# Two-layer encoder trunk: where the second layer's memory keys and values are projected

## Chip, core and metric

The kernel runs on one core of a Trainium2 chip. The metric is device time in microseconds (us) of one execution; three runs of the kernel before gave 1487.01, 1487.39 and 1491.83 us, a median of 1487.39 us. A profiled execution stands beside them. TensorE (PE) is the matrix engine, VectorE (DVE), ScalarE (ACT) and GpSimd (POOL) are the elementwise engines, and SyncE (SP) issues the DMAs named here.

## What is computed

Two pre-norm layers on 1024 tokens of width 1024. Each layer projects its normalised input to queries, keys, values and gates, attends over the tokens, attends over 256 memory tokens with 4 heads of 128, gates, projects out and adds the residual. The part that the change touches is the memory's:

```python
memn = rmsnorm(mem, mem_norm_gain)            # (1, 256, 1024)
for l in range(DEPTH):                        # 2 layers
    mk, mv = jnp.split(memn @ w_mem_kv[l], 2, axis=-1)   # 4 heads of 128 each
    ...
    ym = memory_attn(qm, mk, mv)
```

Both layers use the same normalised memory with their own 1024x1024 weights. So the second layer's `mk` and `mv` depend on nothing of the first layer and can be made at any time before the second layer's memory attention.

## The kernel before

**Arithmetic.** All matmuls are fp32r. An fp32 operand is split in two: a high part (a rounded copy, ACT) and a low part (the operand less its high part, DVE or POOL), and each product is three matmuls: high x high, high x low, low x high. Weights come in units of 256 KB (128 x 512 fp32): a load into a `wraw` buffer (four of them), a copy to `wh`, a subtraction to `wl` (four of each; `wload`, `wunit`, `wparts`, lines 135 to 161). With `wsplit = ("act", "both")` the subtractions go to DVE and POOL in turn (`either`, L1284). One unit feeds 12 matmuls of 256 columns (keys) or 6 of 512 columns (values).

**Stages.** *prep* (`project_a`, L936) loads the tokens and the memory, scales them by the gains and splits them, projects A-attention's keys, values and queries and rotates them (`rope`, L857), and takes the rows' root mean squares from a second copy of the tokens (`stats`, L809, tiles `xt`). It also projects both layers' memory keys and values: first layer `mem_keys` L987 and `mem_values` L989, second layer L1003 and L1014 (the matmuls are recorded at L561 for keys and at L590 for values, for both layers). These use the memory times its gain but not yet divided by its root mean square; that factor (`rows_m` along columns, `rs_m` along rows) is applied when the results are evicted (L570, L597), and the high and low parts are stored to `kvd[0]` and `kvd[1]` in HBM. *l0* is the first layer's attention, *out0* its output projection. *front*, the stage of sums (L1550), projects the second layer's inputs by a Winograd scheme: pairs of 128 output columns with seven products of 12 matmuls (x, z, then y, x, y, x, z; all recorded at L1619), whose weights are sums and differences of four 256 KB quarters (tiles `wq`, eight buffers; L1667) and whose results are added up in tiles `P` (six buffers) and stored through `yb` (two buffers) or, for gates, directly. Ten pairs go in the order 0, 1, 2, 4, ..., 9, 3; the first four have x and z done early, so that pair 3, the last, has five products left. *l1* is the second layer's attention; it loads `kvd[1]` head by head (`odd`, L2006, recorded as `k<-kv` at L1021), and its matmuls are kept in program order. *out1* ends the kernel.

**What sets the order.** Instructions are put in order on each engine before the run by a scheduler that simulates the engines: it goes by program order, raised by the offsets in `AHEAD` (in *front* weights are raised by 100, evictions by 500, sinks by 20), and by when it believes operands to be ready. At run time every engine, and SP's DMA queue, works in that fixed order. A tile of a tag takes its buffers in turn, so the next tile waits until the oldest buffer's last reader is done.

Of the kernel before, what the change touches and what calls it, by code (L numbers as in the profile page):

```python
# [9 lines left out]
F32 = mybir.dt.float32  # L10
F32R = mybir.dt.float32r
I32 = mybir.dt.int32
AF = mybir.ActivationFunctionType
OP = mybir.AluOpType
# [6 lines left out]
KT = 8  # L21
MEM = 256
EPS = 1e-6
NEG = -1e30
UNIT = 4
PLAN = "xv.xx.V1V1V2V1V1V1V2V1V1V1V2V1V1V1V2V1x2z2V1V1V2V1V1V1V2V1V1V1V2V1V1V1V2V1z4z2z2"
# [21 lines left out]
            c=(("P", "P"), ("P", "P"), ("P", "P"), ("yb", "yb"))),  # L48
       dict(y=(("P", "P", "q", "q", "v"), ("k", "k", "k", "k", "q", "q"), ("H",) * 6, ("H",) * 6, ("P", "P", "q", "q", "v"),
               ("k", "k", "k", "k", "q", "q"), ("H",) * 6),  # L50
            c=(("H", "H"), ("H", "H"), ("mk", "sg"), ("yb", "yb"))))
# [13 lines left out]
class Trunk:  # L65
# [61 lines left out]
    def split(self, h, l, src):  # L127
        self.copy(h, src)
        self.nc.vector.tensor_tensor(l, src, h, op=OP.subtract)
# [805 lines left out]

    def project_a(self, qa, ks, v, qd, mem_h, kvd):  # L936

# [33 lines left out]
        for i in range(9):  # L971
            nc.tensor.matmul(p[i % 2], warm[:, :128], warm, start=True, stop=True)
        w0, w1m = io["w_mem0"], io["w_mem1"]
        mem_l = self.st("mem", [128, KT, MEM], F32R, pool=self.xp)
# [11 lines left out]
        self.wsplit = ("act", "dve")  # L986
        end = [self.mem_keys(w0, mem, kvd[0], ("pj", "tr"), "so", "rt1")]  # L987
        self.wsplit = ("act", "both")
        end.append(self.mem_values(w0, mem, kvd[0], "so"))  # L989
        self.rope_tables()  # L990
# [6 lines left out]
        self.loaded = None  # L997
        self.along_columns(self.rows_m, self.rs_m)
        for e in end:
            e()  # L1000
        for q in range(2):
            after(self.k_unit(units[q], q, ks, v))
        self.mem_keys(w1m, mem, kvd[1], ("tr", "tr"), "so", "rt1")()  # L1003
        self.stats(range(4, 8))
# [6 lines left out]
        for q in range(4):  # L1011
            after(self.q_unit(self.a_unit(w2, q), q, 2, qa, qd))
            if q == 1:
                self.mem_values(w1m, mem, kvd[1], "so")()  # L1014
        while late:
# [533 lines left out]

    def front(self, w, pairs, order, values, plan, x1, squares, dests):  # L1550

# [3 lines left out]
        nc, tc = self.nc, self.tc  # L1555
# [90 lines left out]
        def finish(x, z, n1, tag, e=v):  # L1646

            with self.ahead("evict" if tag == "wq" else "sink"):
# [3 lines left out]
                end(n1, 0, c, e)  # L1652

        def raw(j):
            raw = [self.st("wq", [128, 512]) for _ in range(4)]
            with self.ahead("w"):
                for i, t in enumerate(raw):
                    nc.sync.dma_start(t, w[pairs[j][i // 2]][:, 512 * (i % 2):512 * (i % 2) + 512])
            return raw
# [58 lines left out]
        early = len(xs)  # L1718
        for j in order:
            n1, n2 = pairs[j]  # L1720
            if j:
# [41 lines left out]
    def build(self):  # L1763
        nc, tc, io = self.nc, self.tc, self.io
        with ExitStack() as ctx:
# [17 lines left out]
            def dram(n, name, shape=(128, T)):  # L1783
                return [self.dr.tile(list(shape), F32, name=f"{name}{k}") for k in range(n)]
# [5 lines left out]
            self.vec = nc.vector  # L1790
            kvd = dram(2, "kv", (4, 128, 4, MEM))
            x1d = dram(8, "x1_")
            qd = self.dr.tile([4, 2, 128, T], F32, name="qa")
# [16 lines left out]
            with self.phase("prep", ("act", "dve"), "right", p_pj=5, p_tr=3, rp=2, so=4, x=6, xt=3, rt1=2, rt2=1, rqn=1,  # L1810
                            rss=3, ah=4, al=4, xv=3, xp=2, q=4, k=4):
                self.pools = {"q": early}
                with tc.tile_pool(name="start", bufs=1, reuse_waits="tile", side="right") as self.xp:
                    mq = self.project_a(qa, ka, va, qd, mem_h, kvd)

# [40 lines left out]
            with self.phase("front", ("act", "dve"), t1=8, t2=8, t3=8, t4=8, wq=8, vt=2, P=6, yb=2, p_x=5, p_y=1, p_pv=1, p_tr=1):  # L1856
# [17 lines left out]
                v2 = values()  # L1874
                self.front(wo, pairs, (0, 1, 2, 4, 5, 6, 7, 8, 9, 3), v2, PLAN, x1, rows1, dests)
            self.pools = {}
# [350 lines left out]
```

## Time and profile before

| | |
|---|---|
| three runs | 1487.01, 1487.39, 1491.83 us (median 1487.39) |
| profiled execution, own time | 1488.39 us |
| its span, first to last instruction | 1486.6 us |
| mean granted TensorE clock | 0.998 (1.00 in all stretches below: the 2.4 GHz level) |
| instructions | 25518 |

The profile gives each engine's busy time, groups of instructions by line, who waited for whom, a timeline, and the issue and landing of DMAs. Matmuls are pipelined: one is listed with its whole duration while the next starts sooner, so the pace is read from the start-to-start distance of a chain. Times in windows are microseconds from the first instruction. In this execution prep's own matmuls end near 144 us and *front* runs from about 773 to 1017.7 us.

### The profile page before, as it was taken

To read this page: it belongs to the slowest core of one execution; us is meant where nothing else is said; L and a number is where in the kernel's file an instruction comes from. 1 tells how busy PE (TensorE), PEld (TensorE's weight loads), DVE (VectorE), ACT (ScalarE), POOL (GpSimd) and SP (SyncE) were. 2 spreads that over 40 slices of the span, in tenths; PEclk is the share of its full clock that TensorE was granted. 3 is DMA by queue.
4 is the path that set the end of the run, shared out by engine and by line. 5 is a ranking of instruction groups with operands and counts; after the bars stand their busy time and mean duration, and the time that the engine had idled before them with its cause. 6 is when DMAs were issued, how large, how long until landed. Compare 5 with 4: busy or idle time off the path is not lost.

```text
span 1486.6 us, 25518 instructions
## 1 busy us (share of the span) xinstructions
PE 1465.6 (99%) x8433; PEld 1275.1 (86%) x8433; DVE 1034.8 (70%) x2124; ACT 837.9 (56%) x1877; POOL 642.2 (43%) x767
## 2 busy tenths in 40 slices
PE   9899999999999999999999999999999999999998
PEld 8798888988888788888879887888998888888886
DVE  6687777777776578776687776654446787778674
ACT  7743665556655366655444444444446777777454
POOL 1223568556765656553450000001425556664454
PEclk9999999999999999999999999999999999999999
DMA  8966334334343524378553343567665568788834
GB/s 286 306 159 183 118 119 162 114 128 137 115 139 106 172 76 141 106 265 310 185 181 128 128 140 136 157 169 245 229 245 173 187 195 272 235 287 316 315 107 144
DMA packets 173860, 271.92 MB, mean 183 GB/s; under 512 B 15648, under 2 KB 96800, under 8 KB 172704
## 3 DMA queue, kind: packets, MB, share of 16 engines
q1 hardware_dynamic: 173296, 270.20, 56.2%
q8 instruction: 67, 1.10, 0.3%
q14 instruction: 65, 0.53, 0.1%
q10 hardware_dynamic: 432, 0.09, 0.0%
HBM read 174.28 MB, written 83.89 MB: 174 GB/s over the span
## 4 chain that ended last, share of the span: by engine, by line
PE 85%; DMA 5%; DVE 4%; issue 2%; ACT 2%; POOL 2%; SPq 0%; POOLq 0%; DVEq 0%; ACTq 0%
PE pj L242 15%; PE pj L62 11%; PE x L1619 7%; PE tr L133 6%; PE pv L1068 4%; PE y L1619 4%; PE pv L62 3%; PE s L62 3%; PE pj L1334 3%; PE tr L62 3%; PE sa L1334 2%; PE pv L1619 2%; PE sa L1035 2%; PE sa L1036 2%; PE s L1334 2%
## 5 line engine op out<-in xcount | busy, mean ns | idle before, releaser
L542 DVE TENSOR_TENSOR pl<-tr,ph 128x512 fp32r<-128x512 f32 (+2 forms) x352 | 204.1, 594 | 45.0 <-ACT ph L125 43.0
L242 PE MATMUL pj<-H,wh 128*128 128x512 f32 x704 | 233.7, 412 | 0.5 <-DVE vt L313 0.2
L125 ACT ACTIVATE ph<-tr 128x512 fp32r<-128x512 f32 (+2 forms) x352 | 176.3, 522 | 100.5 <-PE tr L133 76.4
L158 POOL TENSOR_SCALAR wh<-wraw 128x512 fp32r<-128x512 f32 x48 | 32.6, 682 | 275.9 <-PE x L1619 234.0
L125 ACT ACTIVATE wh<-wraw 128x384 fp32r<-128x384 f32 (+1 forms) x163 | 89.0, 553 | 99.4 <-DMA wraw<-w_mem 12.9
L242 PE MATMUL pj<-H,wl 128*128 128x512 f32 x352 | 139.1, 395 | 0.0
L242 PEld LDWEIGHTS pj<-H,wh 128*128 128x128 f32 x704 | 120.2, 189 | 18.3 <-POOL wh L158 1.1
L62 PE MATMUL pj<-H,wh 128*128 128x512 f32 x384 | 121.0, 396 | 0.0
L1121 POOL TENSOR_SCALAR pn<-pn,st 128x384 f32<-128x384 f32 (+1 forms) x128 | 72.4, 567 | 104.7 <-DVE st L1120 69.0
L133 PE MATMUL tr<-ident,P 128*128 128x128 f32 x752 | 115.4, 273 | 0.7 <-DVE pl L542 0.4
L1281 POOL TENSOR_TENSOR wl<-wraw,wh 128x384 fp32r<-128x384 f32 x56 | 63.2, 1130 | 91.4 <-ACT wh L125 85.6
L1119 ACT ACTIVATE pn<-pn,st 128x384 f32<-128x384 f32 (+1 forms) x128 | 75.1, 587 | 42.2 <-DVE st L1116 41.0
L133 PEld LDWEIGHTS tr<-ident,P 128*128 128x128 f32 x752 | 88.9, 140 | 9.1 <-DVE pl L542 1.4
L1041 ACT ACTIVATE P<-sa,st 128x1024 f32<-128x1024 f32 x64 | 71.5, 1117 | 35.3 <-PE tr L133 19.1
L1043 POOL TENSOR_SCALAR P<-P,st 128x1024 f32<-128x1024 f32 x64 | 74.0, 1159 | 32.3 <-DVE st L1042 32.3
L1040 DVE TENSOR_REDUCE st<-sa 128x1 f32<-128x1024 f32 x64 | 77.5, 1219 | 8.3 <-PE sa L1036 7.9
L62 PE MATMUL s<-k,q 128*128 128x384 f32 (+1 forms) x352 | 81.2, 327 | 0.0
L242 PEld LDWEIGHTS pj<-H,wl 128*128 128x128 f32 x352 | 66.2, 188 | 15.3
L62 PE MATMUL pj<-H,wl 128*128 128x512 f32 x192 | 75.6, 394 | 0.0
L160 POOL TENSOR_TENSOR wl<-wraw,wh 128x512 fp32r<-128x512 f32 x52 | 68.7, 1324 | 10.9 <-ACT wh L125 8.4
L62 PEld LDWEIGHTS pj<-H,wh 128*128 128x128 f32 x384 | 66.6, 188 | 5.4
L853 PE MATMUL pj<-ah,H 128*128 128x256 f32 x384 | 70.5, 281 | 0.0
(569 smaller groups left out, 4187.1 us busy)
## 6 DMA issues: line engine op xcount, KB each, us to landing
wraw<-w_o SPq DMA_DIRECT2D x52, 256.0 KB, 4.1
y<-yb SPq DMA_DIRECT2D x24, 512.0 KB, 3.2
wraw<-s SPq DMA_DIRECT2D x64, 192.0 KB, 3.7
wraw<-w_e SPq DMA_DIRECT2D x44, 256.0 KB, 3.2
k<-k SPq DMA_DIRECT2D x42, 256.0 KB, 5.4
s<-bias SPq DMA_DIRECT2D x56, 192.0 KB, 2.0
wq<-w_o SPq DMA_DIRECT2D x40, 256.0 KB, 3.4
y<-sg SPq DMA_DIRECT2D x18, 512.0 KB, 3.3
```

The source lines that it names most:

```text
L62: return lambda *a, **k: self.tc.keep_in_program_order(getattr(self.engine, name)(*a, **k))
L125: return self.nc.scalar.activation(out, in_, AF.Copy, scale=scale)
L133: self.turned = self.fence = self.pe.transpose(o, i, self.ident)
L242: self.pe.matmul(a[:, :n], s[:, kt % UNIT, :], m, start=(kt == 0 and i == 0), stop=(kt == KT - 1 and i == 2))
L542: self.low = nc.vector.tensor_tensor(pl[:, :n], tr[:, :n], ph[:, :n], op=OP.subtract)
L1040: nc.vector.tensor_reduce(st[:, 0:1], s, axis=AX.X, op=OP.max, negate=True)
L1041: nc.scalar.activation(pt, s, AF.Exp, bias=st[:, 0:1], accum_out=st[:, 1:2])
L1043: self.normal = nc.gpsimd.tensor_scalar(pt, pt, st[:, 2:3], 0.5, op0=OP.mult, op1=OP.mult)
L1119: nc.scalar.activation(o, o, AF.Exp, bias=st[:, 0:1], scale=-1.0, accum_out=st[:, 2:3])
L1121: self.normal = normal = nc.gpsimd.tensor_scalar(o, o, st[:, 3:4], 0.5, op0=OP.mult, op1=OP.mult)
L1334: last = nc.tensor.matmul(bank, s[:, k, :], y[3 * u + k][m][:, cols], start=start and u + k + e == 0, stop=u == 1 and k + e == 4, skip_gro ...
L1619: self.last = nc.tensor.matmul(bank, ws[s][:, k, :], b[k][m], start=start and k + i == 0, stop=k == UNIT - 1 and i == 2, skip_group_check= ...
```

## The change

The second layer's projections leave `project_a`. The only trace they leave in prep is one store of `rows_m` (128 x 256, 128 KB) to HBM. In *front* a new function `memory()` is called ahead of the last pair (pair 3). It loads that row tile and the memory again, multiplies them on POOL, splits the normalised memory into high and low parts in four `P` tiles, runs the same 96 key matmuls and 48 value matmuls, evicts them through `yb` (the root mean square being in already, without a multiplication), and stores them to `kvd[1]`.

```diff
-    def project_a(self, qa, ks, v, qd, mem_h, kvd):
+    def project_a(self, qa, ks, v, qd, mem_h, kvd, rmd):
...
         self.along_columns(self.rows_m, self.rs_m)
+        nc.sync.dma_start(rmd, self.rows_m)
         for e in end:
             e()
         for q in range(2):
             after(self.k_unit(units[q], q, ks, v))
-        self.mem_keys(w1m, mem, kvd[1], ("tr", "tr"), "so", "rt1")()
         self.stats(range(4, 8))
...
         for q in range(4):
             after(self.q_unit(self.a_unit(w2, q), q, 2, qa, qd))
-            if q == 1:
-                self.mem_values(w1m, mem, kvd[1], "so")()
...
+        def memory():
+
+            w = self.io["w_mem1"]
+            hs, ls = ([self.st("P", [128, 4, MEM], F32R) for _ in range(2)] for _ in range(2))
+            rows = self.st("vt", [128, 512])[:, :MEM]
+            nc.sync.dma_start(rows, rmd)
+            mem = []
+            for kp in range(4):
+                h, l = (t[kp // 2][:, 2 * (kp % 2):2 * (kp % 2) + 2, :] for t in (hs, ls))
+                x = self.st("wq", [128, 512]).rearrange("p (a n) -> p a n", a=2)
+                nc.sync.dma_start(x, self.io["mq"][kp].rearrange("p (a n) -> p a n", a=2))
+                nc.gpsimd.tensor_tensor(x, x, rows[:, None, :].to_broadcast([128, 2, MEM]), op=OP.mult)
+                for i in range(2):
+                    self.with_gain(x[:, i, :], 16 + 2 * kp + i, h[:, i, :], l[:, i, :])
+                    mem.append((h[:, i, :], l[:, i, :]))
+            self.wsplit = ("act", "both")
+
+            def split(p):
+                o = self.st("yb", [128, 2, 512], F32R)
+                with self.ahead("evict"):
+                    self.copy(o[:, 0, :], p)
+                    nc.vector.tensor_tensor(o[:, 1, :], p, o[:, 0, :], op=OP.subtract)
+                return o.bitcast(F32)
+            for t in range(0, 4, 2):
+                p = self.ps("x")
+                for i in range(2):
+                    for u in range(KT // UNIT):
+                        ws = self.wunit(w[t + i, :, u * UNIT * 128:(u + 1) * UNIT * 128])
...
+                                self.last = nc.tensor.matmul(p[:, i * MEM:(i + 1) * MEM], ws[a][:, k, :], mem[u * UNIT + k][b],
...
+                o = split(p)
+                for e in range(2):
+                    nc.sync.dma_start(kvd[t:t + 2, :, e, :].rearrange("h p n -> p h n"),
+                                      o[:, e, :].rearrange("p (h n) -> p h n", h=2))
+            ps = [self.ps("x") for _ in range(2)]
+            for kt in range(KT):
+                ws = [t.rearrange("p a b -> p (a b)")
+                      for t in self.wunit(w[4:8, :, kt * 128:(kt + 1) * 128].rearrange("h p n -> p h n"))]
...
+            self.wsplit = ("act", "dve")
...
         for j in order:
+            if j == order[-1]:
+                memory()
```

## Rows read from the trace of the kernel before

**Rows 1.** The page: busy time by engine, and the chain's shares by engine.

```profile
PE 1465.6 (99%) x8433; PEld 1275.1 (86%) x8433; DVE 1034.8 (70%) x2124; ACT 837.9 (56%) x1877; POOL 642.2 (43%) x767
...
PE 85%; DMA 5%; DVE 4%; issue 2%; ACT 2%; POOL 2%; SPq 0%; POOLq 0%; DVEq 0%; ACTq 0%
```

**Rows 2.** Busy time by stretch: prep up to 144.3, front from 959.6, then l1.

```profile
core 0: us, PE busy (x) PEld busy (x) DVE busy (x) ACT busy (x) POOL busy (x), PEclk, DMA share, GB/s
28.80:63.90 35.10, 31.25 (x203) 27.39 (x202) 19.85 (x54) 25.59 (x67) 14.35 (x12) 1.00 0.95 311
63.90:80.00 16.10, 15.31 (x129) 15.11 (x128) 10.17 (x26) 8.82 (x23) 0.42 (x1) 1.00 0.84 260
80.00:105.50 25.50, 25.50 (x221) 25.50 (x220) 22.40 (x62) 11.20 (x25) 7.44 (x6) 1.00 0.66 162
105.50:122.00 16.50, 15.51 (x82) 12.41 (x81) 16.29 (x37) 7.39 (x15) 4.22 (x3) 1.00 0.55 147
122.00:144.30 22.30, 22.30 (x145) 20.09 (x144) 13.63 (x31) 4.63 (x10) 6.50 (x7) 1.00 0.70 190
...
959.60:979.10 19.50, 19.50 (x86) 15.81 (x84) 12.28 (x19) 8.57 (x15) 0.00 (x0) 1.00 0.61 163
979.10:1003.70 24.60, 24.60 (x107) 19.97 (x106) 15.33 (x24) 10.48 (x19) 0.00 (x0) 1.00 0.52 141
1003.70:1017.70 14.00, 14.00 (x62) 11.34 (x61) 5.43 (x8) 4.92 (x9) 3.83 (x4) 1.00 0.51 146
```

**Rows 3.** Waits of PE in 64 to 146 us: total, times, longest.

```profile
PE pj L590 <- DVE wl L160: 1.0, 3, 0.6
PE tr L561 <- ACT wh L125: 0.8, 1, 0.8
```

**Rows 4.** The chain in order of time (start, us, what): the pace of matmuls.

```profile
77.46 2.60 PE tr L561 x22
...
920.70 7.90 PE x L1619 x34
```

**Rows 5.** DVE groups, 62 to 125 us, by shape: count, busy us, mean ns.

```profile
L160 DVE TENSOR_TENSOR wl<-wraw,wh 128x512 fp32r<-128x512 f32 x18 | 15.2, 856 | 6.9 <-ACT wh L125 6.9
L884 DVE TENSOR_TENSOR rt<-rqn,c_sinq 128x256 f32<-128x256 f32 x12 | 4.5, 415 | 0.0
```

**Rows 6.** Low parts of weights, ns min/median/max: L160, and front's own, L1281.

```profile
L160 POOL TENSOR_TENSOR wl<-wraw,wh x52: 1271/1292/2293, 43.2 to 1049.0; 128x512 fp32r<-128x512 f32 x52
L160 DVE TENSOR_TENSOR wl<-wraw,wh x30: 677/692/1780, 26.5 to 121.0; 128x512 fp32r<-128x512 f32 x30
...
L1281 DVE TENSOR_TENSOR wl<-wq,wh x53: 683/691/695, 837.9 to 1007.6; 128x512 fp32r<-128x512 f32 x53
```

**Rows 7.** DMA issues (count, KB, median us to landing): 85 to 125, then 930 to 1030.

```profile
wraw<-w_mem SPq DMA_DIRECT2D x8, 256.0 KB, 4.9
...
wraw<-w_o SPq DMA_DIRECT2D x10, 256.0 KB, 4.4
```

**Rows 8.** Timeline at the end of pair 9: when its results leave PE and `P`.

```profile
1003.70 0.63 ACT L125 ACTIVATE wh<-wq 128x512 fp32r<-128x512 f32 x1 [2.10 <-PE x L1619]
1003.96 0.62 PE L1619 MATMUL y<-t,wh 128*128 128x512 f32 x2
1006.35 1.34 DVE L1639 SCALAR_TENSOR_TENSOR yb<-P,yb 128x512 fp32r<-128x512 f32 x2
```

**Rows 9.** Timeline after front: l1's load of memory keys, and its first scores.

```profile
1021.21 0.40 SPq L1021 DMA_DIRECT2D k<-kv  x1
...
1028.82 0.87 PE L62 MATMUL s<-k,q 128*128 128x256 f32 x6
```

**Rows 10.** Timeline, POOL and DVE near 94 us (start, us, engine, line).

```profile
94.36 1.69 POOL L887 TENSOR_TENSOR rp<-rt,rt 128x512 f32<-128x512 f32 x1 [1.44 <-DVE iq_y L785]
...
94.82 1.77 DVE L160 TENSOR_TENSOR wl<-wraw,wh 128x512 fp32r<-128x512 f32 x1
```

More of the change, by code (lines that the diff above doesn't have):

```diff
@@ L972, in project_a @@
             nc.tensor.matmul(p[i % 2], warm[:, :128], warm, start=True, stop=True)
-        w0, w1m = io["w_mem0"], io["w_mem1"]
+        w0 = io["w_mem0"]
         mem_l = self.st("mem", [128, KT, MEM], F32R, pool=self.xp)
@@ L986, in project_a @@
         self.wsplit = ("act", "dve")
-        end = [self.mem_keys(w0, mem, kvd[0], ("pj", "tr"), "so", "rt1")]
+        end = [self.mem_keys(w0, mem, kvd, ("pj", "tr"), "so", "rt1")]
         self.wsplit = ("act", "both")
-        end.append(self.mem_values(w0, mem, kvd[0], "so"))
+        end.append(self.mem_values(w0, mem, kvd, "so"))
         self.rope_tables()
@@ L1548, in finish, with front @@
         list(scale(1))
-    def front(self, w, pairs, order, values, plan, x1, squares, dests):
+    def front(self, w, pairs, order, values, plan, x1, squares, dests, kvd, rmd):
         nc, tc = self.nc, self.tc
@@ L1652, in finish @@
                 end(n1, 0, c, e)
+        def memory():
[24 more added lines that the diff above has]
+                        ws = self.wunit(w[t + i, :, u * UNIT * 128:(u + 1) * UNIT * 128])
+                        for k in range(UNIT):
+                            for e, (a, b) in enumerate(((0, 0), (0, 1), (1, 0))):
+                                self.last = nc.tensor.matmul(p[:, i * MEM:(i + 1) * MEM], ws[a][:, k, :], mem[u * UNIT + k][b],
+                                                             start=i + u + k + e == 0, stop=u * UNIT + k == KT - 1 and e == 2,
+                                                             skip_group_check=True)
+                o = split(p)
[6 more added lines that the diff above has]
+                      for t in self.wunit(w[4:8, :, kt * 128:(kt + 1) * 128].rearrange("h p n -> p h n"))]
+                for c in range(2):
+                    for i, (a, b) in enumerate(((0, 0), (0, 1), (1, 0))):
+                        self.last = nc.tensor.matmul(ps[c], mem[kt][a][:, c * 128:(c + 1) * 128], ws[b],
+                                                     start=kt + i == 0, stop=kt == KT - 1 and i == 2)
+            for c, p in enumerate(ps):
+                o = split(p)
+                for i in range(2):
+                    nc.sync.dma_start(kvd[:, :, 2 + i, c * 128:(c + 1) * 128].rearrange("h p d -> p h d"),
+                                      o[:, i, :].rearrange("p (h d) -> p h d", h=4))
+            self.wsplit = ("act", "dve")
@@ L1791, in build @@
             kvd = dram(2, "kv", (4, 128, 4, MEM))
+            rmd, = dram(1, "rm", (128, MEM))
             x1d = dram(8, "x1_")
@@ L1813, in build @@
                 with tc.tile_pool(name="start", bufs=1, reuse_waits="tile", side="right") as self.xp:
-                    mq = self.project_a(qa, ka, va, qd, mem_h, kvd)
+                    mq = self.project_a(qa, ka, va, qd, mem_h, kvd[0], rmd)
             mid = E(ExitStack())
@@ L1874, in build @@
                 v2 = values()
-                self.front(wo, pairs, (0, 1, 2, 4, 5, 6, 7, 8, 9, 3), v2, PLAN, x1, rows1, dests)
+                self.front(wo, pairs, (0, 1, 2, 4, 5, 6, 7, 8, 9, 3), v2, PLAN, x1, rows1, dests, kvd[1], rmd)
             self.pools = {}
```

## The prediction

> **What bounds the kernel now.** I read the page first: PE is busy for 1465.6 us of a span of 1486.6 us, and 85% of the chain that ended last is PE [rows 1]. So the kernel ends when PE has done its matmuls, and only two things can move the time: the number of columns PE streams, and the 21 us in which it stands still. Next the windows by stretch [rows 2]: PE is busy throughout from 80 to 105.5, from 122 to 144.3 and in the three stretches of front; it idles 3.85 us in 28.8 to 63.9 (35.10 - 31.25), 0.79 us in 63.9 to 80 and 0.99 us in 105.5 to 122. The list of waits tells whose the last two are: 1.0 us of values matmuls waiting for a low part, 0.8 us of keys matmuls waiting for a high part [rows 3]. Both are the very work that moves. The reader is to see that the moved work is not in anybody's way as a whole: it is PE work among PE work, and its own supply is what stalls it. The granted clock is 1.00 in every stretch [rows 2], so it plays no part.
>
> **The change part by part.** *PE work moved.* Before and after there are 96 key matmuls of 256 columns and 48 value matmuls of 512. 22 of the former take 2.60 us, 0.118 each; 34 of the latter 7.90 us, 0.232 each [rows 4]. So 96 x 0.118 + 48 x 0.232 = 11.3 + 11.1 = 22.4 us leave prep and come back in front. PE has no free time there (24.60 of 24.60 and 14.00 of 14.00 busy [rows 2]), so nothing hides them: the two terms cancel, and the result is a sum of small stalls.
>
> *Stalls that leave prep.* The two waits of [rows 3] go: -1.8 us. The bounds are 0 (something else then waits in their place) and -5.6, all of PE's idle time from 28.8 on (3.85 + 0.79 + 0.99). I take -1.8, the waits that belong to the moved lines.
>
> *Stalls that come to prep.* The moved work is also a filler: PE runs keys while the second half of the statistics loads and rotations are awaited. What is late next is DVE. From 63.9 to 122 it is busy 48.9 us of 58.1, 84% [rows 2]. Of 18 low parts in that stretch (15.2 us [rows 5]) 16 are the second layer's, 13.5 us; the four eviction passes by DVE on the keys and two on the values are 6 x 0.69 = 4 us at the duration of a 512-wide pass [rows 6]. That leaves about 31 us of DVE work against 58.1 - 1.8 - 22.4 = 34 us of PE: 92%, so DVE has less slack than before. If it needs its old slack (31 / 0.84 = 37), 3 us are lost; if the projection after it (122 to 144.3, DVE 13.6 of 22.3 busy [rows 2]) serves as the new filler, nothing is. I take +1.0, nearer to zero because five accumulators let PE run ahead of the rotations. SP gains too: 16 loads (4 MB) and 8 stores go, one store of 128 KB comes, and the `xt` loads that share the queue with the key weights can only be earlier.
>
> *The supply in front.* The 16 weight units need, per `wraw` buffer, a landing of 4.4 to 4.9 us [rows 7], a high part of 0.63 us on ACT [rows 8] and a low part of 0.69 us on DVE or 1.29 us on POOL [rows 6]: 5.7 to 6.8 us, over four buffers 1.43 to 1.70 us per unit, while PE uses a unit in 12 x 0.118 = 1.42 us. So there is a deficit of 0 to 0.28 us per unit, 0 to 4.5 us in all 16, less what is loaded and split ahead (four buffers of each kind, so up to eight units). I take +1.8, what the same 16 units cost in prep [rows 3]. DMA has room: its share is 0.51 to 0.61 in front [rows 2], where 1 MB of memory, 4 MB of weights and 2 MB of stores come in (29 issues on SP, all behind pair 9's stores in one queue).
>
> *The memory's halves.* The four `P` tiles take buffers of pairs 8 and 9 in turn. The last one needs the buffer that pair 9 frees when its DVE split of `yb` ends, at 1007.7 (1006.35 + 1.34), while PE finishes pair 9 at 1003.96 [rows 8]. So the low halves of the last four 128-row blocks are late by 3.7 us and their four DVE passes of about 0.42 us [rows 5], a bound of 5.4; against it, the first units of four heads (4 x 1.42 us) need only the early halves and can be run first, which gives 0. I take +0.8, nearest to the row where such reordering was possible throughout, front's stretches without idle time [rows 2].
>
> *What I cost at nothing.* POOL's four multiplications (4 x 1.29 us [rows 6]) are hidden by pair 9, since POOL does nothing from 959.6 to 1003.7 [rows 2]; without that cover they would delay the first key by 5.2 us. ACT has 10.48 of 24.60 us busy [rows 2] and takes 16 high parts (10 us), eight halves and four evictions. The new wait is l1's: `k<-kv`, issued at 1021.21 now, must find the values stored, and the query loads and four weight loads are queued behind it on SP; its scores start at 1028.82 [rows 9]. Pair 3's 14.0 us of products [rows 2] stand between, so the stores (one eviction and a landing, some 5 us by [rows 7]) are over in time. Should memory be the very last thing in front, that wait would show.
>
> Sum: -1.8 + 1.0 + 1.8 + 0.8 = +1.8 us. The profiled execution took 1488.39 us for a span of 1486.6, that is 1.0 above the median of the runs; on the median, 1487.39 + 1.8 = **1489.2 us**.
>
> **A row against a rule.** In prep a low part on DVE has a median of 692 ns and a maximum of 1780, in front 691 and 695, where POOL stands idle [rows 6]; the one that began at 94.82, inside a POOL operation that ran from 94.36 to 96.05, took 1.77 us [rows 10]. So a DVE pass that meets a POOL pass waits for its end, and the change brings POOL into front. The Trainium skill (SBUF — State Buffer, "Who interferes with whom") says the same more sharply: a DVE instruction with two SBUF inputs and a GpSimd instruction that reads SBUF exclude each other for the whole instruction. By that rule the trace agrees, and all 12 POOL passes of the new stretch would be closed time for DVE's two-input passes; this speaks against the change, and is the first rival.
>
> **The rivals.** *DVE and POOL shut each other out in front (slower).* Place: the low parts of memory and weights. POOL's 12 passes (four multiplications, eight low parts in turn) are 12 x 1.29 = 15.5 us; DVE's two-input passes are eight low parts (5.5), eight memory halves (3.4) and pair 3's four sums (2.8), 11.7 us [rows 5, 6]. Together 27.2 us against 22.4 us of PE: 4.8 us late, 1489.2 + 4.8 = 1494.0 us. It decides if the scheduler starts them no earlier than the stretch; for it speaks 1.77 us [rows 10], against it that DVE has 9 us free in the 24.6 us before [rows 2], where half of this can be done. Chance 0.17. *Prep does not shrink in full.* DVE keeps its old slack and costs 3 us, and the statistics chain that keys covered costs as much again as the 1.6 us not in [rows 3]: 4.6 in place of 1.0, and 1492.8 us. For it: 16.29 of 16.50 us DVE [rows 2]. Against: PE runs ahead. Chance 0.14. *Prep was held by its loads (faster).* DMA share 0.95 and 0.84 [rows 2] up to 80 us; 4 MB less lets PE's idle 5.6 us vanish, and front is fed in time: 1487.39 - 5.6 = 1481.8 us. Against: 3.85 of the 5.6 lie before 63.9, ahead of most moved loads. Chance 0.12. *It doesn't do what it says:* the scheduler spreads memory's units over pairs 8 and 9, all stalls are filled and prep's gain and loss cancel, 1487.4 us; chance 0.07. The forecast has the remaining 0.50.
>
> **How the numbers follow.** A measurement of this kernel can tell some 0.3%, 4.5 us, from no change: 1482.9 and 1491.9. Faster: the third rival almost whole, 0.12. Slower: most of the first two (0.13 + 0.09) and the upper end of the forecast, where supply and halves reach their bounds (0.06): 0.28. The rest, 0.60, is no change. The range takes in the faster rival's upper part and the first rival with some of the supply's bound: 1482.5 to 1496.0; both signs hold chance, so the forecast's own range stands beside it, 1485 to 1493.
>
> **What would show it.** Right: prep's last matmul near 144.3 - 22.4 - 0.8 = 121 us; no idle PE of over 1 us in 64 to 122; front longer by 22.4 plus 2 to 3 us, with the idle time before key and value matmuls and `wh` or `wl` as releaser. Wrong by the first rival: waits of PE for `wl` with DVE low parts of over 1.5 us in front. Wrong by the second: prep ends at 125 or later, PE waiting for `rp` or the statistics. Wrong by the third: PE's idle time in 28.8 to 63.9 gone. A wait of l1's first scores for `k<-kv` would refute the cover of pair 3.

## The result, and the profile after

The changed kernel takes 1493.23 us in the median of 11 runs (1490.8 to 1498.36), the kernel before beside it 1487.39 us (11 runs); the ratio is 1.0042, with a 95% interval of 1.003 to 1.0054. That is slower by 5.8 us (4.5 to 8.0 by the interval), where the forecast had +1.8 and its own range ended at 1493. The profiled execution took 1496.08 us for a span of 1494.1 us, 7.5 us more than the span before. Lines of the changed kernel are two lower in *front* (L1617 was L1619); the new `memory()` has its key matmuls on L1682 and its value matmuls on L1695.

The page after, against [rows 1]:

```profile
PE 1469.5 (98%) x8433; PEld 1275.8 (85%) x8433; DVE 1039.6 (70%) x2122; ACT 843.1 (56%) x1885; POOL 661.1 (44%) x779
```

PE does the same 8433 matmuls, but its idle time has grown from 21.0 us (1486.6 - 1465.6) to 24.6 us, and 3.9 us are in matmuls that took longer, some of them at a lower clock (below). To see where, one follows the same matmuls through both traces. Groups of matmuls by line give first and last starts; this is the group of l0's first scores, before and then after (a view of one line's instructions: count, ns min/median/max, first to last start):

```profile
L1035 PE MATMUL sa<-k,q x128: 388/393/486, 144.3 to 447.6; 128*128 128x512 f32 x128
```

```profile
L1033 PE MATMUL sa<-k,q x128: 388/393/486, 118.9 to 423.0; 128*128 128x512 f32 x128
```

and this is *front*'s product group, again before and then after:

```profile
L1619 PE MATMUL x<-H,wh x80: 390/392/478, 772.9 to 986.5; 128*128 128x512 f32 x80
...
L1619 PE MATMUL pv<-t,wh x32: 390/393/404, 851.6 to 1017.2; 128*128 128x512 f32 x32
```

```profile
L1617 PE MATMUL x<-H,wh x80: 390/393/477, 751.2 to 966.3; 128*128 128x512 f32 x80
...
L1617 PE MATMUL pv<-t,wh x32: 390/393/404, 831.1 to 1024.1; 128*128 128x512 f32 x32
```

Read as a ledger of how far the changed kernel is ahead of the one before:

| the same matmul | before | after | after less before | step |
|---|---|---|---|---|
| l0's first scores | 144.3 | 118.9 | -25.4 | prep: 22.4 moved, 3.0 gained |
| last of that group | 447.6 | 423.0 | -24.6 | 0.8 given back |
| front's first `x` | 772.9 | 751.2 | -21.7 | 2.9 lost |
| front's first `pv<-t` | 851.6 | 831.1 | -20.5 | 1.2 lost |
| pair 9's last `x<-H` | 986.5 | 966.3 | -20.2 | 0.3 lost |
| pair 3's last `pv<-t`, behind the memory | 1017.2 | 1024.1 | +6.9 | 27.1 for 22.4 of work: 4.7 lost |
| end of the span | 1486.6 | 1494.1 | +7.5 | 0.6 lost |

So prep gave what was forecast and a little more; *front* lost 4.7 us around the memory where I had 2.6 (1.8 + 0.8); and 2.9 us went where I had not looked, between l0 and *front*. The windows after (columns as in [rows 2]) show the places:

```profile
28.80:63.90 35.10, 33.25 (x221) 29.36 (x220) 22.58 (x60) 27.66 (x74) 15.29 (x12) 1.00 0.99 327
63.90:80.00 16.10, 16.10 (x141) 16.10 (x140) 10.36 (x44) 7.02 (x23) 3.31 (x3) 1.00 0.32 97
80.00:97.00 17.00, 16.12 (x138) 15.73 (x137) 16.78 (x36) 4.87 (x11) 6.10 (x4) 1.00 0.82 206
97.00:119.00 22.00, 21.52 (x137) 18.77 (x136) 20.10 (x47) 7.65 (x16) 7.08 (x7) 1.00 0.46 112
...
630.50:634.20 3.70, 1.94 (x8) 1.35 (x7) 3.70 (x5) 0.14 (x1) 1.76 (x2) 0.93 0.48 157
634.20:637.70 3.50, 3.50 (x12) 2.82 (x11) 1.44 (x3) 0.52 (x1) 0.00 (x0) 0.59 0.84 241
960.00:985.10 25.10, 23.76 (x102) 18.77 (x100) 13.35 (x19) 11.56 (x21) 3.69 (x3) 1.00 0.62 181
985.10:998.20 13.10, 12.14 (x97) 11.95 (x97) 7.61 (x16) 7.46 (x15) 3.44 (x3) 1.00 0.62 169
998.20:1010.70 12.50, 12.07 (x51) 8.84 (x50) 9.28 (x11) 6.48 (x11) 5.63 (x4) 1.00 0.77 240
```

In prep PE idles 1.85 + 0 + 0.88 + 0.48 = 3.2 us from 28.8 on, against 5.6 [rows 2]. At 630.5 it idles 1.76 us, and then the granted clock falls: its mean is 0.59 over the next 3.5 us, that is, the lower level (1.2 GHz) for most of them. In the last three windows it idles 2.7 us. The waits name both places (total, times, longest):

```profile
PE sa L1332 <- DVE wl L1279: 1.8, 1, 1.8
...
PE x L1682 <- ACT P L125: 1.4, 1, 1.4
...
PE x L1682 <- DVE P L792: 0.9, 1, 0.9
```

**Around the memory.** PE does not wait for weights there, as I thought it would, but for the memory itself, once for a high half (ACT) and once for a low half (DVE). POOL had multiplied the memory long before, and the timeline of pair 9's end shows why that was of no use (start, us, engine, line, idle before and its releaser):

```profile
958.21 3.42 POOL L1663 TENSOR_TENSOR wq<-wq,vt 128x512 f32<-128x512 f32 x2 [0.71 <-DMA wq<-mq]
```

```profile
984.09 0.58 ACT L125 ACTIVATE P<-x 128x512 f32<-128x512 f32 x1
...
984.57 3.29 ACT L125 ACTIVATE P<-wq,gain 128x256 fp32r<-128x256 f32 x8
984.70 1.28 DVE L1642 TENSOR_TENSOR P<-P,x 128x512 f32<-128x512 f32 x2 [2.53 <-ACT P L125]
...
985.12 0.38 PE L1682 MATMUL x<-P,wh 128*128 128x256 f32 x1 [1.36 <-ACT P L125]
...
985.90 2.86 DVE L792 SCALAR_TENSOR_TENSOR P<-wq,gain,P 128x256 fp32r<-128x256 f32 x7
...
986.44 0.39 PE L1682 MATMUL x<-P,wh 128*128 128x256 f32 x1 [0.94 <-DVE P L792]
```

The last multiplication ends at 961.6. All eight high halves stand on ACT behind the eviction of pair 9's last product (984.09), all low halves on DVE behind that product's two passes. So the first key matmul waits for a result of pair 9 that it does not use.

**At the start of out0.** The same stretch, first before and then after, at the end of l0:

```profile
645.26 1.30 POOL L497 TENSOR_TENSOR sg<-yb,sg 128x512 f32<-128x512 f32 x1 [1.36 <-DMA sg<-y]
...
650.14 2.32 DVE L129 TENSOR_TENSOR H<-H 128x512 fp32r<-128x512 f32 x3
...
651.89 1.73 POOL L499 TENSOR_TENSOR sg<-yb,sg 128x512 f32<-128x512 f32 x1
...
654.09 1.64 DVE L1281 TENSOR_TENSOR wl<-wraw,wh 128x384 fp32r<-128x384 f32 x1
...
655.79 0.50 PE L1334 MATMUL sa<-q,wl 128*128 128x512 f32 x1
```

```profile
621.94 1.29 POOL L497 TENSOR_TENSOR sg<-yb,sg 128x512 f32<-128x512 f32 x1 [3.00 <-DMA sg<-y]
...
625.75 4.24 DVE L129 TENSOR_TENSOR H<-H 128x512 fp32r<-128x512 f32 x3
626.00 1.74 POOL L499 TENSOR_TENSOR sg<-yb,sg 128x512 f32<-128x512 f32 x1
...
627.69 1.76 POOL L502 TENSOR_TENSOR yb<-sg,yb 128x512 f32<-128x512 f32 x1
...
632.73 0.50 PE L1332 MATMUL sa<-q,wl 128*128 128x512 f32 x1 [1.76 <-DVE wl L1279]
```

A 512 KB load of `sg` lands 1.6 us later than before (POOL waits 3.00 us for it, not 1.36). POOL's passes over it then run beside DVE's three passes over `H`, which take 4.24 us in place of 2.32; DVE comes late to a low part that out0's first products need, and PE stands. Out0's first `sa` matmul is 25.0 us ahead of the kernel before (623.7 against 648.7), its first `tr<-q` 21.5 (643.4 against 664.9): 3.5 us went there, 1.8 in the pause and 1.7 in the lower clock behind it. All traces together say the same. From the last of l0's first scores to *front*'s first `x` there are 324.4 to 325.3 us in the six without this wait (before, front_added, before_shift, after_half, halves_early, halves_early_pad; the experiments follow), 325.9 to 327.0 in the three with the wait alone (prep_alone, halves_first, after_pad), and 328.2 and 328.3 in the two where the clock falls too (the changed kernel, all_dve). Those are means of 324.8, 326.5 and 328.3: 1.8 us for the wait, 3.5 with the lower clock. The Trainium skill (SBUF — State Buffer, "Who interferes with whom") has the rule, exclusion for a whole instruction; by it these rows agree.

### The profile page after: what moved, and what is told of

The parts are those of the page before. It is cut to its first block, busy times and chain, and to the rows that moved or that the text cites. A ratio compares the mean times of both kernels' runs of the same rounds, so it can differ in the third digit from the quotient of the medians.

```text
span 1494.1 us, 25561 instructions
## 1 busy us (share of the span) xinstructions
PE 1469.5 (98%) x8433; PEld 1275.8 (85%) x8433; DVE 1039.6 (70%) x2122; ACT 843.1 (56%) x1885; POOL 661.1 (44%) x779
## 4 chain that ended last, share of the span: by engine, by line
PE 50%; DVE 2%; DMA 2%; issue 1%; POOL 1%; ACT 1%; POOLq 0%; DVEq 0%; ACTq 0%
PE pj L62 11%; PE x L1617 6%; PE y L1617 4%; PE pv L62 3%; PE s L62 3%; PE pj L1332 3%; PE tr L62 3%; PE sa L1332 2%; PE pv L1617 2%; PE s L1332 2%; PE tr L1332 2%; PE tr L1345 1%; PE sa L1345 1%; PE pj L1345 1%; PE pv L1332 1%
## 5 line engine op out<-in xcount | busy, mean ns | idle before, releaser
L242 PEld LDWEIGHTS pj<-H,wh 128*128 128x128 f32 x704 | 120.2, 189 | 17.8 <-POOL wh L158 0.6
L160 POOL TENSOR_TENSOR wl<-wraw,wh 128x512 fp32r<-128x512 f32 x60 | 80.7, 1348 | 45.9 <-ACT wh L125 43.0
L1663 POOL TENSOR_TENSOR wq<-wq,vt 128x512 f32<-128x512 f32 x4 | 6.4, 1604 | 201.5 <-DMA wq<-mq 201.3
```

Of the source, the lines that this page charges most:

```text
L160: e.tensor_tensor(lf, raw, hf, op=OP.subtract)
L242: self.pe.matmul(a[:, :n], s[:, kt % UNIT, :], m, start=(kt == 0 and i == 0), stop=(kt == KT - 1 and i == 2))
```

## The experiments

The first four ask which side of the move costs what. **prep_alone** does the first half of the change alone; the second layer's memory projection is left out, and l1 reads the first layer's memory keys and values.

```diff
-            if j == order[-1]:
-                memory()
...
-                first, begun = self.odd(wo, kvd[1], yd[1], vd, mqd, qd, gd)
+                first, begun = self.odd(wo, kvd[0], yd[1], vd, mqd, qd, gd)
```

> The second layer's memory projection is left out everywhere: prep is as in the changed kernel, front as in the kernel before, and the second layer reads the first layer's memory keys and values. It leaves out 22.4 us of PE work, so its time is read against 1487.4 - 22.4 = 1465.0 us. Theory A (prep gives back about 2.5 us more than its work, front loses about 4.7 us): 1462.5 us. Rival C (a shift of prep's end by 25 us also brings the stall at the end of the first layer's attention, 1.8 us of idle PE and 1.6 us of half clock, more often): 1464 to 1466 us, and that stall is seen again in the trace.

1467.87 us, ratio 0.9866 (0.9841 to 0.9891), 19.9 us less than before by the ratio (16.2 to 23.6). Theory A's 1462.5 lies outside that, and the rival's 1464 to 1466 inside; whether less is gained than the 22.4 us of work, the interval leaves open. Its trace has the same wait at out0's start, in a kernel that has nothing of the change in *front*, as the rival foresaw:

```profile
PE sa L1332 <- DVE wl L1279: 1.8, 1, 1.8
```

**front_added** does the other half alone: prep keeps the projection, and *front* does it a second time.

```diff
+        self.mem_keys(w1m, mem, kvd[1], ("tr", "tr"), "so", "rt1")()
...
+            if q == 1:
+                self.mem_values(w1m, mem, kvd[1], "so")()
```

> Prep is as in the kernel before and projects the second layer's memory; front projects it once more, as in the changed kernel. Read against 1487.4 + 22.4 = 1509.8 us. Theory A: front's own stalls, 4.7 us, come on top: 1514.5 us; PE waits for the P tiles ahead of the first keys for over 2 us. Rival B (DVE and POOL shut each other out in front): the same sum, but the waits are for wl behind DVE passes of over 1.5 us. Rival C: nothing is shifted ahead of front, so less of the changed kernel's loss returns here, and the sum of both runs' deviations falls short of 5.8 us.

1515.94 us, ratio 1.0202 (1.0174 to 1.023), 30.0 us more for 22.4 of work. From pair 9's last `x<-H` to pair 3's last `pv<-t` there are 58.8 us (985.7 to 1044.5), 30.7 before: 28.1 for 22.4. As theory A wanted, PE waits for `P` ahead of the keys, 1.4 and 0.9 us. There is no wait at out0's start. Both halves together are 10.1 us beyond their work, more than the 5.8 of the change, but each is uncertain by some 4 us.

**halves_first** and **all_dve** try two causes for the stretch: the halves' place in the order, by the planner's offset, and POOL's part in it.

```diff
+                with self.ahead("norm"):
                     nc.gpsimd.tensor_tensor(x, x, rows[:, None, :].to_broadcast([128, 2, MEM]), op=OP.mult)
                     for i in range(2):
                         self.with_gain(x[:, i, :], 16 + 2 * kp + i, h[:, i, :], l[:, i, :])
```

> The changed kernel with the multiplication and the splitting of the memory raised by 300 in the scheduler's order, so that the halves need not stand behind pair 9's last evictions on ACT and DVE. Theory A: the waits for P ahead of the first and the sixth key matmuls go (1.5 + 1.2 us), 1493.2 - 2.5 = 1490.7 us. Rival B: the POOL passes now meet pair 9's low parts, no gain or 1 to 2 us slower. If the buffers of P bound it and not the order, no change: 1493 us.

1492.94 us, 1.0036 (1.0021 to 1.005): no different from the change. The offset did not do what it was for: the halves still stand behind pair 9's last eviction,

```profile
984.67 0.58 ACT L125 ACTIVATE P<-x 128x512 f32<-128x512 f32 x1
985.15 3.29 ACT L125 ACTIVATE P<-wq,gain 128x256 fp32r<-128x256 f32 x8
```

so this run says nothing of what earlier halves are worth. In the trace the order of computing instructions is the changed kernel's on every engine: it is that kernel once more. Its time is what was expected should the buffers of `P`, and not the order, hold the halves; why the planner left them there is not shown.

```diff
-                nc.gpsimd.tensor_tensor(x, x, rows[:, None, :].to_broadcast([128, 2, MEM]), op=OP.mult)
+                nc.vector.tensor_tensor(x, x, rows[:, None, :].to_broadcast([128, 2, MEM]), op=OP.mult)
...
-            self.wsplit = ("act", "both")
+            self.wsplit = ("act", "dve")
```

> The changed kernel with the memory's multiplication and all 16 low parts on DVE, so that POOL does nothing in this stretch of front. Rival B: the closed time goes, 2 to 4 us faster than the changed kernel, 1490 us. Theory A: the halves stay behind pair 9's evictions, no gain: 1492 to 1494 us, DVE passes of the stretch all near 0.69 us.

1492.04 us, 1.0032 (1.0019 to 1.0044), which overlaps with the change. The waits for `P` are as long as before, only those for `wl` are gone:

```profile
PE x L1682 <- ACT P L125: 1.4, 1, 1.4
PE x L1682 <- DVE P L792: 1.1, 1, 1.1
```

So exclusion between DVE and POOL is not what makes the halves late. The stretch is as long as the change's, 57.9 us, though the granted clock fell behind these two waits. The same window of all_dve, of halves_first and of the changed kernel:

```profile
986.70:990.10 3.40, 3.40 (x16) 3.40 (x17) 3.40 (x9) 2.95 (x7) 0.00 (x0) 0.50 0.14 48
...
986.70:990.10 3.40, 3.08 (x13) 2.84 (x14) 3.40 (x9) 3.17 (x8) 0.00 (x0) 0.58 0.26 86
...
986.70:990.10 3.40, 3.40 (x28) 3.40 (x28) 3.40 (x9) 3.14 (x7) 0.00 (x0) 1.00 0.23 76
```

The pair to compare is all_dve and halves_first, both with the fall: 57.9 us without POOL and 58.0 with it, so POOL's passes cost the stretch nothing that shows. Nor does the fall cost much there: from 986.7 the changed kernel has done 98 matmuls at 998.4 and halves_first 82, but at 1011.0 148 and 146, since the changed kernel waits for `wl` in between (0.5 us) and halves_first does not.

**halves_early** puts the loads and halves ahead of pair 9's last product in program order, and makes room for them: two of a pair's `P` tiles share one buffer.

```diff
-            c22, c12, c21 = (self.st("P", [128, 512]) for _ in range(3))
+            both = self.st("P", [128, 2, 512])
+            c22, c12, c21 = both[:, 0, :], both[:, 1, :], self.st("P", [128, 512])
...
             u = unit(a21)
             more(40)
+            if j == order[-2]:
+                mem = halves()
             product(x, u, t3, False)
```

> The changed kernel with the loads, multiplications and halves of the memory written ahead of pair 9's last product instead of behind it, and two of a pair's three P tiles laid into one, so that the four P tiles of the memory reuse tiles that come free before pair 9 ends. Theory M (the eight halves, ordered behind pair 9's last evictions, cost 1.5 us ahead of the first key matmul and 1.2 us in the first unit, of the 4.7 us by which the stretch exceeds its 22.4 us of work): no wait for P ahead of the key matmuls, the stretch is 24.4 us instead of 27.1, and the time is 2.0 to 2.7 us less than the changed kernel's: 1490.5 to 1491.2. Rival S (the supply of low halves sets the pace of the keys, and the halves were only ahead of it in the queue): the same waits come back with wh or wl as the releaser, the stretch is 26 us or more, and the time falls by less than 1 us.

1489.4 us, 1.001 (0.9999 to 1.002). The order is now the one wanted, the high halves beginning seven us ahead of the first key matmul (978.0), and what is left of the waits is the supply of weights:

```profile
970.64 3.30 ACT L125 ACTIVATE P<-wq,gain 128x256 fp32r<-128x256 f32 x8
...
981.55 0.58 ACT L125 ACTIVATE P<-x 128x512 f32<-128x512 f32 x1
```

```profile
PE x L1699 <- POOL wl L160: 0.6, 1, 0.6
PE x L1699 <- ACT wh L125: 0.6, 1, 0.6
```

The stretch is 55.2 us (963.6 to 1018.8), 24.5 for the memory in place of 27.1. Theory M is shown, at 2.6 us, with place and room changed together. By the ratios the time fell by 4.8 us, some 2.4 either way. This profile also has no wait at out0's start, but that is not the edit's doing: up to about 975 us the computing instructions of each engine come in the changed kernel's order.

That wait is what the other seven runs are about. Theory F: a packet of TensorE's instructions comes by the DMA engines inside the load of `sg` and delays it. **after_pad**, **after_half** and **before_shift** change how many instructions TensorE has ahead of it, by the warming matmuls at the very start (and with them the length of the start):

```diff
-        for i in range(9):
-            nc.tensor.matmul(p[i % 2], warm[:, :128], warm, start=True, stop=True)
+        for i in range(25):
+            nc.tensor.matmul(p[i % 2][:, :184], warm[:, :128], warm[:, :184], start=True, stop=True)
```

> The changed kernel with 25 warming matmuls of 184 columns in place of 9 of 512 at the start (about the same columns), so that TensorE has 32 instructions more ahead of everything else. In all four traces without the second projection in the preparation a 16 KB packet of instructions lies inside the 0.5 MB load of sg at the end of l0, which then lands 6.1 to 6.4 us after its issue; in the two with it (before, front_added) the packet lies elsewhere and the load lands after 4.3 to 4.8 us. Theory F (the fetch of TensorE's instructions, which comes about every 256 of them, was moved into that load because 288 instructions of TensorE are gone ahead of it): 32 more put it back where it was, the load lands within 5 us, the wait of 1.8 us at out0's start and the half clock behind it go, and the time is 1.9 to 3.4 us below the changed kernel's 1493.2: 1489.8 to 1491.3. Rival T (the shorter preparation itself, or chance, set the transfers against each other): the load still lands after 6 us or more, the wait of 1.7 to 1.8 us stays, and the time is 1492.5 to 1494.

1496.43 us, 1.0055 (1.0039 to 1.0071), above what either gave. The load landed after 6.4 us and the wait stayed (1.7 us): as the rival said, though the packet had moved only to the load's beginning (617.11 to 618.49 us, the load's issue at 617.30). **after_half** has `range(73)`, 16 rows and 64 columns instead:

> The changed kernel with 73 warming matmuls of 16 rows and 64 columns in place of 9 of 512, that is 128 instructions of TensorE more, half of the 256 between two fetches. In after_pad (32 more) the packet of instructions moved only to the beginning of sg's load, took 1.4 us there, and the load still landed after 6.4 us. Theory F: with the packet some 10 us away the load lands within 4.8 us as in the two traces of a packet ahead of it, and the wait at out0's start is gone. Rival T: it lands after 5.5 us or more without a packet in it, and the fetch is not what holds it. What the start loses by the added matmuls (in before_shift 112 of them cost 23 us there) is not judged: the trace from the end of l0 decides.

Its time, 1499.69 us in one run, is not judged. Here theory F's outcome came. The queues over the life of that load, in the changed kernel and then here (queue, kind, packets, MB, share of 16 engines; the last line is the load itself):

```profile
q1 hardware_dynamic: 687, 1.79, 90.9%
q8 instruction: 1, 0.02, 0.9%
```

```profile
q1 hardware_dynamic: 447, 1.35, 88.6%
...
sg<-y SPq DMA_DIRECT2D x1, 512.0 KB, 5.0
```

With no packet of instructions in it the load lands after 5.0 us (4.8 was expected), and no wait comes. One packet is 0.9% of 16 x 6.42 us, 0.9 us on one of the 16 engines. **before_shift** (the kernel before, `range(121)`, 38 columns) is the converse:

> The kernel before with 121 warming matmuls of 38 columns in place of 9 of 512: 224 instructions of TensorE more, which is 32 fewer up to a multiple of 256, the shift that the change brings to the fetches; the preparation keeps all of its work. Theory F: a 16 KB packet of instructions falls inside the load of sg at the end of l0, the load lands 6 us or more after its issue instead of 4.8, and TensorE waits some 1.8 us for wl at out0's start though nothing of the change is made. Rival T: no packet there matters, the load lands after 4.5 to 5 us, and no wait over 0.5 us comes at out0's start. The 121 matmuls take 4.2 us as the nine did if columns set their pace, up to some 8 us if each has a floor of its own, so the time is 1487 + 0 to 4, and by theory F 1.9 to 3.4 more; what decides is the landing and the wait.

1506.2 us, 1.0138 (1.0119 to 1.0157); the warming matmuls alone took 21.9 us longer, where 0 to 4 had been expected, and 18.3 of it are left at l0's first scores (162.6 against 144.3). With a packet inside, the load landed after 5.6 us, 0.8 later than before, and yet no wait came: neither theory's outcome. **after_swap** and **before_swap** take the load ahead of the store that it queued behind:

```diff
-        nc.sync.dma_start(dst[:, 0:2, :], two(y))
         nc.sync.dma_start(two(sg), yd[k - 6][:, 0:2, :])
+        nc.sync.dma_start(dst[:, 0:2, :], two(y))
```

> The changed kernel with the load of sg put ahead of the store of y beside it (two lines exchanged), wherever that code runs. Theory L (TensorE's wait of 1.8 us at the start of out0 follows from that load: it lands 6.1 to 6.4 us after its issue behind the store, GpSimd's three passes over sg then meet VectorE's three passes over H, and the low halves come late): the load lands some 3 us after its issue, as the store did that stood first, the wait falls below 0.5 us, the half clock behind it does not come, and the time is 1.9 to 3.4 us below the changed kernel's 1493.2: 1489.8 to 1491.3. Rival C (the meeting of the passes has another cause, such as the products of l0 that end then, or the store, now late, holds the loads of y behind it): a wait of over 1 us stays at that place, under this releaser or another, and the time is 1492.5 to 1494.5.

> The kernel before with the same exchange of two lines. Theory L: there the load landed after 4.8 us and TensorE did not wait, so nothing is to be gained: 1487 with 0.5 either way. Rival: the exchange is a gain or a loss of its own at the seven other places where this code runs, and the time moves by 1 us or more, which then has to be taken off the result of the changed kernel too.

After: 1493.52 us, 1.0043 (1.003 to 1.0056). The load lands after 4.2 us, and the wait shrinks to 0.6 us, and the clock does not fall behind it; it was to fall below 0.5. But the time is the change's; here the clock fell behind the waits for `P`, from 985.4. Before: 1487.84 us, 1.0014 (1.0002 to 1.0027): the exchange costs some 2 us (0.3 to 4.0) of its own, and has a wait of 0.7 us where there was none. Theory L holds for the wait and fails as a remedy; less that cost after_swap would be some 2 us better than the change, which the intervals don't tell from nothing. **halves_early_swap** and **halves_early_pad** combine:

> The earlier halves and the exchange of load and store in one. In halves_early the load of sg landed after 5.6 us and no wait came at out0's start, so theory L lets its profile gain nothing there; in runs in which it lands later it takes that chance away. Expected 1487.5 to 1489.5 (halves_early: 1489.4, its runs from 1485.7 to 1493.4); a time above 1490 speaks for a loss at the other places.

1490.23 us, 1.0022 (1.0008 to 1.0035): above the range that was expected and above halves_early, as the swap's own cost would have it, but the two intervals overlap.

> Both edits together, the earlier halves and the 25 warming matmuls. If theories F and M both hold, the two gains add up: 1493.2 less 1.9 to 3.4 less 2.0 to 2.7 is 1487.1 to 1489.3, which is the kernel before within what can be told apart, and leaves of the change nothing but the exchange of work. If only one holds, 1489.8 to 1491.3. If neither, 1492.5 to 1494.

1492.72 us, 1.0035 (1.0023 to 1.0047), the range for neither theory, though its trace shows both effects (a stretch of 55.2 us, no wait). Against halves_early it is 0.6 us behind at front's first `x` (750.6 against 750.0), 1.4 at pair 3's last `pv<-t` and 3.3 at the end: lost in small pieces that no experiment here follows. The padding seems to have a cost of its own: by the ratios after_pad is 1.9 us above the change, and this kernel 3.7 above halves_early.

Three pairs of kernels differ in the halves alone: the change and halves_early, the two padded, the two exchanged. By the ratios the early halves gain 4.8, 3.0 and 3.1 us, and in the traces the stretch falls from 57.8, 58.3 and 57.9 us to 55.2, 55.2 and 54.2. So theory M doesn't rest on one pair.

The load and the wait in all fourteen traces (in us; the landing is that of the `sg` load from its issue):

| kernel | landing | wait at out0's start | memory's stretch |
|---|---|---|---|
| before | 4.8 | none | 30.7 |
| front_added | 4.3 | none | 58.8 |
| before_shift | 5.6 | none | 30.7 |
| after | 6.4 | 1.8 | 57.8 |
| prep_alone | 6.4 | 1.8 | 30.7 |
| halves_first | 6.2 | 1.7 | 58.0 |
| all_dve | 6.1 | 1.8 | 57.9 |
| after_pad | 6.4 | 1.7 | 58.3 |
| after_half | 5.0 | none | 58.4 |
| halves_early | 5.6 | none | 55.2 |
| halves_early_pad | 5.7 | none | 55.2 |
| before_swap | 4.1 | 0.7 | 30.8 |
| after_swap | 4.2 | 0.6 | 57.9 |
| halves_early_swap | 4.0 | 0.4 | 54.2 |

Where the load is second in the queue, the wait is there at 6.1 us and above and not at 5.7 and below. No version that does all the work beats the kernel before; halves_early equals it within the interval.

## Why the prediction was right or wrong

*PE work moved: right.* 22.4 us left prep and came back; the ledger has no other large term.

*Stalls that leave prep and come to it (-1.8 and +1.0): right in sum.* The profiled pair has -3.0 at l0's first scores and -2.2 at the last of them. Over the traces the last of these scores stands at 447.6, 447.1 and 446.9 with the projection (before, before_swap, front_added) and at 423.0, 424.9, 425.5, 424.3, 425.0, 425.4 and 422.6 without it and without added warming matmuls: means of 447.2 and 424.4, a gain of 22.8, so -0.4 beyond the work against -0.8 forecast. The profiled pair lies at one end of that scatter. DVE is the tight engine as foreseen (16.78 of 17.00 us busy in 80 to 97), but PE loses only 0.88 us there. At the first scores the means are 143.3 and 120.2, a gain of 23.1, so -0.7.

*The supply in front (+1.8): right.* With the halves out of the way, halves_early shows 24.5 - 22.4 = 2.1 us, of which 1.2 are waits for `wh` and `wl`.

*The memory's halves (+0.8): the term that was mis-sized; it is 2.6.* I bounded it by the buffer that the last `P` tile needs, which touches the last four blocks, and took a low value because PE can reorder. What happened is coarser: all eight halves were ordered behind pair 9's last evictions, on two engines, though their inputs were ready 23 us earlier (961.6 against 984.57). PE cannot reorder around that, since every key matmul needs a half. halves_early measures it by removing it: the sum had the term 1.8 us too small.

*What I costed at nothing.* POOL's multiplications were hidden (over by 961.6, so the memory's loads did not stand behind pair 9's stores, as I had written), and l1's load of `k<-kv` was: issued at 1028.21, scores at 1035.75, no wait between. But I costed everything from l0 to *front* at nothing without naming what could move there. A load came late at a place where 0.1 us was to spare (before, the low part ended at 655.73, 654.09 + 1.64, and PE used it at 655.79). In the changed kernel a packet of instructions comes in the midst of that load, 3.9 us after its issue; in before it comes 0.5 us ahead of the issue and ends about when the load's first data move. after_half, one run, has the load early again without a packet; before_shift shows that one alone need not be enough, and after_pad that the load can be late with the packet at its beginning. So that the load's lateness makes most of the wait is shown (after_swap, after_half); that the packet makes the load late is likely and not shown. The price is 1.8 us of waiting and, in two traces, 1.7 us more at the lower clock. This is the second part of the miss: +1.8 with 2.6 in place of 0.8 is 3.6, and 1.8 to 3.5 from here make it 5.4 to 7.1, for 5.8 measured. The wait is known from one execution of each kernel; halves_early has none after the same instructions, so how often it comes is not known. The profiled pair has 2.1 us more in small pieces (1.2, 0.3 and 0.6 in the ledger) that no run here follows.

*The range.* 1493.23 lies past my own mark for no change (1491.9), where I had put 0.28, and just past the forecast's own 1493. It lies within the wide range, but that end was there for the first rival and for the bounds of supply and halves; a loss that the prediction did not name took their place, so that the range held is in part luck.

*The rivals.* The first came nearest in time (1494.0) and is refuted in its mechanism: without any POOL pass in the stretch (all_dve) the same two waits for `P` stand, 2.5 us together, and the stretch is as long as in halves_first, which has POOL's passes. Exclusion did bite, at out0's start, where the change put no new pass. The second (prep does not shrink in full) is refuted by the scores at 118.9, which I had put at 121 and 125. The third saw prep's idle time in 28.8 to 63.9 fall from 3.85 to 1.85 us, half of what it wanted, but was swallowed by the losses. The scheduler did not spread the units: the key matmuls stand in one block from 985.1 to 998.2.

**What stays open.** What makes that load late. Where a packet lies inside it, its place goes with the delay: begun 3.0 and 3.6 us after the load's issue (halves_early, before_shift) the load landed after 5.6 us, begun 3.7 to 4.4 us after it (halves_first, the changed kernel, all_dve, prep_alone) after 6.1 to 6.4. Where it lay across the load's beginning, the load landed after 4.3 and 4.8 us (front_added, before) and after 5.7 and 6.4 (halves_early_pad, after_pad). Open too is what the 1.2 us between front's first `x` and its first `pv<-t` are; after, two waits of 0.4 and 0.3 us for DVE's evictions lie there that before has not. Neither was tried, nor was what keeps the planner from putting the halves earlier.

## What to carry to other kernels

When work is moved into a stage, ask of each of its operands on each engine which instruction it stands behind, not only when its input and buffer are ready: here a result that nobody needed yet cost 2.6 us. Then look for the places in the stages between that have next to no slack, because moving work shifts everything that follows, and a load that lands 1.6 us later there is paid for. And a profile of each kernel is one draw: by the end of l0, prep's gain was 2.2 us in the pair and 0.4 us over ten traces, and halves_first, the same instructions in the same order, has the lower clock at another place than the changed kernel.

## What the hardware showed that I had not expected

Instructions come by the same DMA engines as the data. The page of the changed kernel lists its queues (packets, MB, share of 16 engines):

```profile
q8 instruction: 67, 1.10, 0.3%
```

Queue 8's are 16 KB each, one for some 250 of PE's 16,866 matmuls and weight loads; no other engine has so many instructions, so I take them for PE's. Where one fell into the midst of that 512 KB load, the load landed after 5.6 to 6.4 us, where none came near it after 5.0 us (after_half), and where one lay across its beginning after 4.3 to 6.4 us. The Trainium skill (Runtime: NRT & Kernel Launch, "Instruction fetch mechanics") states blocks of that size and calls their cost mostly hidden; the size agrees. What a fetch costs the engine that fetches, no run here shows; that it can cost a load beside it is what these rows suggest.

The granted clock can fall after a short pause, and need not. PE stood 1.8 us at out0's start, and the clock fell in the changed kernel and in all_dve, but not in prep_alone after a pause of the same length (its windows, the pause and what follows, columns as in [rows 2]):

```profile
632.60:635.80 3.20, 1.45 (x7) 1.00 (x6) 3.20 (x4) 0.17 (x1) 1.79 (x2) 1.00 0.44 165
635.80:639.20 3.40, 3.40 (x20) 2.87 (x19) 2.14 (x5) 1.12 (x2) 0.00 (x0) 1.00 0.79 217
```

Behind the waits ahead of the key matmuls it fell in six of the seven traces with late halves (front_added, halves_first, all_dve, after_pad, after_half, after_swap), and not in the seventh, the changed kernel.

A small matmul can cost as much as its weight load. Each warming matmul has one of its own. The 121 of 38 columns at the start of before_shift took as long as the first line says, the nine of 512 columns of the kernel before as the second:

```profile
1.31 26.00 PE L972 MATMUL pj<-rp 128*128 128x38 f32 x121 [1.31 <-POOL rp L968]
```

```profile
1.31 4.09 PE L972 MATMUL pj<-rp 128*128 128x512 f32 x9 [1.31 <-POOL rp L968]
```

That is 0.21 us for each of the former and 0.45 for the latter, for 13 times the columns. after_pad's 25 of 184 columns took 5.64 us, 0.23 each. But after_half's 73 of 64 columns, with weights of 16 columns in place of 128, took 4.06 us, 0.056 each. So it is not the number of instructions that made before_shift's start long, but 121 loads of 128 columns of weights.
